# Input and output products of the S5 mixer in other slots, and the last adaLN pieces inside the S5 half of the out-projection

## The chip, the cores and the metric

The kernel runs on 1 core of a Trainium2 chip. The metric is the device time of that core in microseconds (us). The engines are named as in the profile: PE (TensorE matrix products), DVE (VectorE), ACT (ScalarE), POOL (GpSimd) and SP (SyncE, which in this kernel issues nearly all DMAs from one queue, in order).

## The reference

One layer of a diffusion backbone on 640 tokens (128 context, 512 latent) of 2048 columns, all float32. Cut to what matters:

```
mod = silu(c) @ w_ada + b_ada                  # 6 x 2048 columns, for c_ctx and for c
h = rmsnorm(x) * (1 + scale_m) + shift_m
u_a, v_a, u_b = split(h @ w_in)                # 3 x 1024 columns
y_a = u_a * (w_s @ rmsnorm(v_a) + b_s)         # chunk mixer, 8 heads
h_t = lam_bar * h_(t-1) + b_bar @ u_b          # S5: 64 groups of 16 channels, complex
y_b = gelu(Re(c @ h) + d * u_b)                #   states of 64, both directions
y_b = y_b * sigmoid(y_b @ w_glu + b_glu)
mix = [rmsnorm(y_a), rmsnorm(y_b)] @ w_out
x = x + gate_m * rmsnorm(mix)
f = relu(modulate(rmsnorm(x), scale_f, shift_f) @ w_ff1)**2 @ w_ff2
x = x + gate_f * rmsnorm(f)
```

## The kernel before

Most products run as three matrix products of split operands (hi times hi, hi times lo, lo times hi), so each weight chunk is loaded by SP (`wr`), rounded by ACT (`wh`) and subtracted by DVE (`wl`) before PE can take all of it. The modulation (adaLN) is computed in 16 columns (m, c) for gate_m, scale_f, shift_f and gate_f, each of four 1 MB pieces of `w_ada` and a closing step; one call of `ada_step` does one of these (tiles `aw` of 0.5 MB, three buffers, all products of one piece into `adaq`; the closing step makes `adap`).

After a first part (modulation of the input, the S5 quarter `ub` of the in-projection, whose results go to DRAM as `ud`, L322) the program is a hand-written sequence of slots (`slot()`, L488, where every engine keeps the order of the code; the traces give its instructions line 443, since one wrapper issues them). A slot runs its phases in this order: SP loads the chunk after next, `evac`, ACT rounds the next chunk, `act`, `dve`, a first quota of a background flow, DVE subtracts for the next chunk and PE multiplies this one, `pe`, a second quota of the flow, `end`. `at(t, phase, f)` puts a piece of work into slot t. The quotas are in estimated microseconds; the flow is a generator that yields an estimate after each DVE operation.

- Slots 0 to 15: the v columns of the in-projection (48 products of 320 columns a slot, `ws`). The flow is `tables()`: the powers of lam_bar times b, c for 16 units of four groups (`unit(u)`), DVE products on tables St, O and t out of the table tile `big`; small copies ks get two DVE additions a unit, and the results go to DRAM (sd, od, kd).
- Slots 16 to 31: the u columns. `s5_in(u)`, 16 products (`x1p`) a unit, in slots 17 to 21; then the flow is the scan (`scan()`, DVE: scq, sct, X). The chunk mixer follows (vc, z, zt), and its result is stored to DRAM (`yad`) and read back as `ya`.
- Slot 32 has no main chunk. Slots 33 to 48 are the chunk-mixer half of the out-projection (16 chunks of 30 products of 512 columns, `as`).
- Then `s5_out(u)`, 24 products (`yp`) a unit, two units a slot; `y_store` sends y to DRAM (`yd`), `yc_load` reads it back in another layout, `gelu(k)` does GELU (w, yb) and splits the result (yb parts); then 8 chunks of the GLU product.
- `out_b` (L1194): the S5 half of the out-projection (`ob`), for three blocks of tokens (G1) and then two (G2), with the second norm and its transposes (`tp`) between and behind. Here the compiler's scheduler sets the order, no longer the slots. The FFN (L1304) follows and is not touched.

Tiles at the place of the change:

```
w = pa.tile([128, 2, 512], F32, name="aw", tag="aw", bufs=3)      # 0.5 MB each
slot(True, 3.0, 10.0)          # quotas of the flow in slots 0 to 15
```

Of the kernel before, what the change touches and what calls it, by code (L numbers as in the profile page):

```python
# [43 lines left out]
def build(nc, tc, a, out, tap=None):  # L44
# [930 lines left out]
    ya_ = {}  # L975

    def ya_load(k):
        ya_[k] = pbs["pb"].tile([128, L * NJ], F32, name="ya", tag=("ya", "vc")[k % 2], bufs=1)
        SY.dma_start(ya_[k][:, 0:NT], yad[k * 128:(k + 1) * 128])
# [12 lines left out]
    for k, (tl_, pl, ts, ps__) in enumerate(((31, "sp", 31, "end"), (31, "end", 32, "act"), (32, "sp", 33, "act"),  # L992
                                             (33, "sp", 33, "end"), (33, "end", 34, "act"), (34, "sp", 34, "end"))):
        at(tl_, pl, lambda k=k: ya_load(k))
        at(ts, ps__, lambda k=k: split(ya_[k][:, 0:NT], k, g_oa[:, k:k + 1], yah, yal))
# [685 lines left out]
```

## Time and profile before

The three timed runs have a median of 2857.01 us (2856.06 to 2859.68).

| | us |
|---|---|
| profiled execution, its own time | 2859.06 |
| its span, first to last instruction | 2857.2 |
| PE busy | 2661.9 (93%) |
| DVE busy | 1950.0 (68%) |
| ACT busy | 1099.3 (38%) |
| POOL busy | 40.0 (1%) |

The share of the chain that ended last is 77% PE, 9% DVE, 8% DMA. The kernel was read by stages:

| stretch, us | what runs |
|---|---|
| 237.52 to 443.13 | slots 0 to 15, the tables |
| 443.13 to 543.49 | slots 16 to 21 |
| 543.49 to 632.38 | slots 22 to 30 |
| 632.38 to 691.28 | slots 31 to 35 |
| 691.28 to 757.00 | slots 36 to 43 |
| 757.00 to 833.24 | slots 44 to 48, S5 output units 0 to 3 |
| 833.24 to 908.71 | S5 output units 4 to 15 |
| 908.71 to 962.85 | y through DRAM, the last GELU |
| 962.85 to 1021.75 | GLU product |
| 1021.75 to 1222.96 | `out_b`, second norm, transposes |
| 1222.96 to 2857.20 | FFN |

In a row of a stretch stand its bounds, its length, then the busy time with the number of instructions (x) of PE, PEld, DVE, ACT and POOL, the mean granted clock of TensorE (1 is 2.4 GHz, 0.5 is 1.2 GHz), the mean busy share of the 16 DMA engines, and GB/s. In a row of a timeline "[9.77 <-DMA ...]" is the time the engine stood idle ahead of the instruction and what ended it. A row joins xN like instructions, and its length goes from the first start to the last end. A busy matmul row is not a sum to add up: matmuls overlap, so lengths of whole rows or stretches are used.

### The profile page before, as it was taken

Reading aid. Unit: us, or ns where it says so; the run is one execution under the profiler, and the core shown is the slowest. Engines: PE = TensorE matmul, PEld = TensorE weight load, DVE = VectorE, ACT = ScalarE, POOL = GpSimd, SP = SyncE. Lnnn points to the kernel's source line nnn. Section 1 sums busy time; section 2 is a strip of 40 time slices with the busy share of each in tenths; the row PEclk is TensorE's granted clock in tenths of the full one; section 3 lists DMA queues with packets and bytes.
Section 4 is the critical chain, followed back from the end, with each engine's and each line's share of the span. In section 5 each row is a group of like instructions: output and inputs, shape, how many; then the busy total and the mean of one; then the engine's idle time right before and its main releaser. Section 6 shows DMA issues by size and latency. Waiting matters only on the chain.

```text
span 2857.2 us, 42969 instructions
## 1 busy us (share of the span) xinstructions
PE 2661.9 (93%) x17217; PEld 2447.7 (86%) x17217; DVE 1950.0 (68%) x2872; ACT 1099.3 (38%) x1755; POOL 40.0 (1%) x33
## 2 busy tenths in 40 slices
PE   8997888998987898789999999999899999999997
PEld 5687777985665676689999999999899999999996
DVE  5566991478802546677777777777567777777776
ACT  4121321212211334755555555555433222323343
POOL 0000000000000100000000000000000000000000
PEclk9998998999995899899999999999999999999998
DMA  9845779654578565335655555565754455356453
GB/s 304 284 157 203 230 242 222 203 169 171 180 221 174 179 213 206 96 101 176 184 175 178 177 180 178 176 183 177 260 210 147 160 218 200 117 191 219 159 188 114
DMA packets 466567, 537.40 MB, mean 188 GB/s; under 512 B 35216, under 2 KB 378160, under 8 KB 458688
## 3 DMA queue, kind: packets, MB, share of 16 engines
q1 hardware_dynamic: 453264, 528.55, 57.4%
q10 hardware_dynamic: 13104, 6.10, 1.1%
q8 instruction: 136, 2.23, 0.3%
q14 instruction: 63, 0.52, 0.1%
HBM read 417.78 MB, written 116.80 MB: 187 GB/s over the span
## 4 chain that ended last, share of the span: by engine, by line
PE 77%; DVE 9%; DMA 8%; ACT 2%; issue 1%; SPq 1%; ACTq 0%; DVEq 0%
PE X L1304 31%; PE Y L1304 16%; PE Z L1304 8%; PE ws L443 5%; PE ub L186 4%; PE as L443 4%; PE ob L1204 3%; DMA aw<-in_w_ada_dram 2%; PE adaq L443 2%; PE ada L196 2%; DVE t L443 2%; DVE O L443 1%; DVE St L443 1%; PE x1p L443 1%; DMA so<-kd 1%
## 5 line engine op out<-in xcount | busy, mean ns | idle before, releaser
L1291 ACT ACTIVATE wh<-wx 128x1024 fp32r<-128x1024 f32 x223 | 235.8, 1057 | 309.7 <-PE X L1304 141.8
L1296 DVE TENSOR_TENSOR wl<-wx,wh 128x1024 fp32r<-128x1024 f32 x223 | 272.8, 1223 | 73.8 <-ACT wh L1291 71.7
L1304 PE MATMUL X<-B,wh 128*128 128x320 f32 x1376 | 306.5, 310 | 3.3 <-ACT wx L1291 3.3
L1304 PEld LDWEIGHTS X<-B,wh 128*128 128x128 f32 x1376 | 232.3, 190 | 3.5 <-ACT wx L1291 3.5
L1304 PE MATMUL X<-B,wl 128*128 128x320 f32 x688 | 213.2, 310 | 0.0
L1304 PE MATMUL Y<-B,wh 128*128 128x320 f32 x672 | 150.9, 312 | 4.3 <-ACT wh L1291 4.3
L1304 PE MATMUL X<-B,wx 128*128 128x320 f32 x1008 | 154.7, 309 | 0.0
L443 PE MATMUL ws<-hTh,wl 128*128 128x320 f32 x512 | 126.2, 330 | 29.6 <-DVE wl L443 29.6
L443 ACT ACTIVATE wh<-wr 128x1024 fp32r<-128x1024 f32 x56 | 59.3, 1058 | 238.8 <-DMA wr<-in_w_in_dram 138.9
L1304 PEld LDWEIGHTS X<-B,wx 128*128 128x128 f32 x1008 | 149.6, 188 | 0.0
L1379 DVE TENSOR_TENSOR wx<-wx 128x320 fp32r<-128x320 f32 x192 | 93.1, 485 | 78.0 <-ACT wx L1376 78.0
L1502 DVE TENSOR_TENSOR facc<-facc,X 128x640 f32<-128x640 f32 x116 | 95.1, 820 | 73.7 <-PE X L1304 72.8
L443 PE MATMUL adaq<-aw,sc 128*32 128x512 f32 x512 | 95.6, 685 | 52.9 <-DMA aw<-in_w_ada_dram 52.3
L1304 PE MATMUL X<-B2n,wh 128*128 128x320 f32 x608 | 134.7, 309 | 0.0
L443 PE MATMUL ws<-hTh,wh 128*128 128x320 f32 x512 | 128.2, 334 | 7.0 <-ACT wh L443 7.0
L1304 PEld LDWEIGHTS X<-B,wl 128*128 128x128 f32 x688 | 130.2, 189 | 0.0
L443 PE MATMUL ws<-hTl,wh 128*128 128x320 f32 x512 | 124.0, 325 | 0.0
L1291 ACT ACTIVATE wh<-wr 128x1024 fp32r<-128x1024 f32 x76 | 80.4, 1058 | 110.4 <-PE X L1304 51.4
L443 PEld LDWEIGHTS ws<-hTh,wl 128*128 128x128 f32 x512 | 92.4, 203 | 33.2 <-DVE wl L443 33.2
L1291 ACT ACTIVATE wx<-wr 128x1024 fp32r<-128x1024 f32 x75 | 79.3, 1058 | 105.9 <-PE X L1304 54.5
L1291 ACT ACTIVATE wx<-wx 128x1024 fp32r<-128x1024 f32 x74 | 78.3, 1058 | 103.8 <-PE X L1304 45.9
L1304 PEld LDWEIGHTS Y<-B,wh 128*128 128x128 f32 x672 | 114.2, 191 | 4.6 <-ACT wh L1291 4.6
(397 smaller groups left out, 6667.8 us busy)
## 6 DMA issues: line engine op xcount, KB each, us to landing
wx<-in_w_ff_dram SPq DMA_DIRECT2D x169, 512.0 KB
x2d<-wx SPq DMA_DIRECT2D x224, 320.0 KB
aw<-in_w_ada_dram SPq DMA_DIRECT2D x128, 512.0 KB
wr<-in_w_ff_dram SPq DMA_DIRECT2D x87, 512.0 KB
was<-in_w_ada_dram SPq DMA_DIRECT2D x64, 512.0 KB
B2n<-x2d SPq DMA_DIRECT2D x24, 1280.0 KB
wr<-in_w_in_dram SPq DMA_DIRECT2D x48, 512.0 KB
wr<-in_w_out_dram SPq DMA_DIRECT2D x48, 512.0 KB
```

The lines of the kernel that those rows point to most:

```text
L186: T.matmul(p[:, :n], st[:, kk, c:c + 128], mv(k)[:, t0:t0 + n], start=(first and i == 0), stop=(last and i == 2))
L196: T.matmul(p[32 * j:32 * j + 32], sc[:, 2 * (k0 + i):2 * (k0 + i) + 32], w[:, i, :], start=k0 + i < 4, stop=k0 + i >= NK - 4)
L443: return lambda *p, **k: P(f(*p, **k))
L1204: T.matmul(p, st[:, k0 + kk, tsl], mv[:, kk, :], start=(k0 + kk == 0 and i == 0), stop=(k0 + kk == 7 and i == 2))
L1291: P(S.activation(hls[n][0], raw, AF.Copy))
L1296: P(V.tensor_sub(lo, raw, hi.bitcast(F32)))
L1304: P(T.matmul(p, st[:, j, c:c + 128], xv(j, x), start=first and j == 0 and i == 0, stop=j == nj - 1 and i == 2, skip_group_check=not first))
L1379: P(V.tensor_sub(hlt[i][:, 1], raw, hlt[i][:, 0].bitcast(F32)))
L1502: P(V.tensor_add(dst, dst, src))
```

## The change

- The `ud` stores go out from POOL's queue. The loads of the b tables stand right behind the first weight chunk on SP's queue, ahead of the `aw` loads.
- The two sign scalings of b2 and c1 go from DVE to ACT; the two DVE operations a unit on ks become three on POOL (128x16 each), and kd is stored a slot earlier.
- The flow's quotas in slots 0 to 15 go from 13 to 11.3, and `ada_step` is left out in every fourth slot there, and in slots 16 to 20, 33, 34 and every fourth slot from 36 on; slot 32 keeps its three calls; the second calls in slots 42 to 48 go.
- `s5_in` takes four units a slot in slots 17 to 20, and the scan starts in slot 21.
- Of the mixer's results only head 0 goes through DRAM; heads 1 to 5 stay in SBUF (`ykeep`), and their splits move to the ends of slots 32 to 34.
- `s5_rest(e)` starts S5 output in the slot after the scan ends; chunks of the out-projection that are left run beside it.
- The split of yb leaves `gelu` and stands in the first GLU slot.
- The last 6 of the 16 adaLN columns (24 pieces of 1 MB and 6 closing steps) leave the slots; `ada_rest` issues one after each half-block step of `out_b`, from two 1 MB buffers `awr`.

The diff, cut:

```diff
-                nc.sync.dma_start(ud[cb * 128:(cb + 1) * 128], us)
+                nc.gpsimd.dma_start(ud[cb * 128:(cb + 1) * 128], us)
...
+    cols_ = [(m, c) for m in (2, 4, 3, 5) for c in range(4)]
+    steps = [(m, c, q) for m, c in cols_[:10] for q in range(5)]
...
     raw_of(0)
+    for i, nm in enumerate(("b1", "b2")):
+        SY.dma_start(btab[:, i, :], a[nm])
     raw_of(1)
     hi_of(0)
     lo_of(0)
-    ada_load()
     d16 = g_.tile([128, 16], F32, name="d16")
     id16 = g_.tile([128, GH], F32, name="id16")
-    for i, nm in enumerate(("b1", "b2")):
-        SY.dma_start(btab[:, i, :], a[nm])
     SY.dma_start(ctab[:, 0, :], a["c1"])
     SY.dma_start(d16, a["ssm_d"])
     SY.dma_start(id16, a["id16"])
+    ada_load()
...
-        V.tensor_scalar(btab[:, 1, :], btab[:, 1, :], sgn, -1.0, op0=OP.mult, op1=OP.mult)
-        yield 1.3
+        S.activation(btab[:, 1, :], btab[:, 1, :], AF.Copy, scale=nsgn)
...
-        V.tensor_scalar(ctab[:, 0, :], ctab[:, 0, :], sgn, None, op0=OP.mult)
-        yield 1.3
+        S.activation(ctab[:, 0, :], ctab[:, 0, :], AF.Copy, scale=sgn)
...
-            at(now[0] + 1, "dve", lambda: (
-                V.tensor_add(ks[:, 7, :], ks[:, 7, :], ks[:, 15, :]),
-                V.scalar_tensor_tensor(ks[:, 7, :], id16, d16[:, u:u + 1], ks[:, 7, :], op0=OP.mult, op1=OP.add)))
-            at(now[0] + 2, "sp", lambda: SY.dma_start(kd[u], ks[:, 0:15].rearrange("p s c -> p (s c)")))
+            G.tensor_add(ks[:, 7, :], ks[:, 7, :], ks[:, 15, :])
+            G.tensor_tensor(ks[:, 15, :], id16, d16[:, u:u + 1].broadcast_to([128, GH]), op=OP.mult)
+            G.tensor_add(ks[:, 7, :], ks[:, 7, :], ks[:, 15, :])
+            at(now[0] + 1, "sp", lambda: SY.dma_start(kd[u], ks[:, 0:15].rearrange("p s c -> p (s c)")))
...
-        ada_step(t)
-        slot(True, 3.0, 10.0)
+        if t % 4 != 3:
+            ada_step(t)
+        slot(True, 2.0, 9.3)
...
+        if 1 <= h < 6:
+            if h % 2:
+                ykeep.append(pbs["pb"].tile([128, 1536], F32, name="yk", tag="so", bufs=3))
+            y_ = ykeep[-1][:, (h + 1) % 2 * NT:(h + 1) % 2 * NT + NT]
         for n in range(2):
-            V.tensor_mul(zt[:, n * 320:(n + 1) * 320], zt[:, n * 320:(n + 1) * 320], bank["u", h][n][:, :320])
+            V.tensor_mul(y_[:, n * 320:(n + 1) * 320], zt[:, n * 320:(n + 1) * 320], bank["u", h][n][:, :320])
+        if h == 0:
+            at(now[0] + 1, "sp", lambda: SY.dma_start(yad, zt))
+            at(now[0] + 3, "sp", ya_load)
...
-    for t, us in ((17, range(0, 3)), (18, range(3, 6)), (19, range(6, 9)), (20, range(9, 12)), (21, range(12, 16))):
-        for u in us:
-            at(t, "pe", lambda u=u: s5_in(u))
+    for u in range(16):
+        at(17 + u // 4, "pe", lambda u=u: s5_in(u))
...
+    for k in range(6):
+        at((32, 32, 32, 33, 33, 34)[k], "end", lambda k=k: split(ya_[k], k, g_oa[:, k:k + 1], yah, yal))
...
+    def yb_split(k):
+        if k == 0:
+            ybs.extend(a20([128, 8, NT], F32R, f"yb{i}") for i in range(2))
         S.activation(yb_part(k, 0), ybk(k), AF.Copy)
         V.tensor_sub(yb_part(k, 1), ybk(k), yb_part(k, 0).bitcast(F32))
...
+    def s5_rest(e):
+        for u in range(16):
+            at(e + u // 2, "pe", lambda u=u: s5_out(u))
+        for half in range(2):
+            at(e + 4 * half + 4, "sp", lambda half=half: y_store(half))
+            for i in range(4):
+                k = 4 * half + i
+                at(e + 4 * half + 5 + i // 2, "sp", lambda k=k: yc_load(k))
+                at(e + 4 * half + 6 + i // 2, "act", lambda k=k: gelu(k))
...
+    e = None
+    t = 16
+    while t < 49 or e is None or t < e + 11:
+        if t == 21:
+            flow[0] = scan()
+        if 35 <= t < 38:
+            at(t, "end", lambda u=t - 35: so_load(u))
+        if scanned and e is None:
+            e = t
+            s5_rest(e)
         if t == 32:
             for _ in range(3):
                 ada_step(t)
-            slot(False, 0, 3.0)
-            continue
-        if t == 22:
-            flow[0] = scan()
-        ada_step(t)
-        if t >= 41 and t % 2 == 0 or t >= 45:
+            slot(False, 0, 0.0)
+        elif t < 49:
+            if 21 <= t < 32 or t > 34 and t % 4:
+                ada_step(t)
+            slot(True, *((0, 0) if t < 21 else (2.0, 4.6) if t < 32 else (0.0, 2.0) if t == 33 else (2.0, 5.0)))
+        else:
             ada_step(t)
-        if 43 <= t < 46:
-            at(t, "end", lambda u=t - 43: so_load(u))
-        slot(True, *((0, 0) if t < 22 else (1.5, 5.0) if t < 32 else (2.0, 5.0)))
-    while not scanned:
-        ada_step(now[0])
-        slot(False, 0, 7.0)
-    e = now[0]
-    for u in range(16):
-        at(e + u // 2, "pe", lambda u=u: s5_out(u))
-    for half in range(2):
-        at(e + 4 * half + 4, "sp", lambda half=half: y_store(half))
-        for i in range(4):
-            k = 4 * half + i
-            at(e + 4 * half + 5 + i // 2, "sp", lambda k=k: yc_load(k))
-            at(e + 4 * half + 6 + i // 2, "act", lambda k=k: gelu(k))
-    for t in range(e, e + 11):
-        ada_step(t)
-        if t >= e + 8:
-            ada_step(t)
-        slot(False)
-    for t in range(e + 11, e + 19):
-        at(t + 1, "evac", lambda cb=t - e - 11: glu_evac(cb))
+            slot(False, 0, 7.0)
+        t += 1
...
+    for k in range(8):
+        at(t, "act", lambda k=k: yb_split(k))
+    for t in range(t, t + 8):
+        at(t + 1, "evac", lambda cb=cur[0] - 48: glu_evac(cb))
         ada_step(t)
         slot(True)
...
+    awr = fc.tile([128, 5, 1024], F32, name="awr", tag="b6", bufs=1)
+    def ada_rest():
+        pieces = [(m, c, q) for m, c in cols_[10:] for q in range(4)]
+        def ld(i):
+            if i < len(pieces):
+                m, c, q = pieces[i]
+                w = awr[:, 2 * (i % 2):2 * (i % 2) + 2].rearrange("p a (b c) -> p (a b) c", c=512)
+                nc.sync.dma_start(w, wada[:, 4 * q:4 * q + 4, m * D + c * 512:m * D + (c + 1) * 512])
+                return w
+        ws = [ld(0), ld(1)]
+        for i, (m, c, q) in enumerate(pieces):
+            if q == 0:
+                p = pq("adaq")
+            ada_mm(p, ws[i], 4 * q)
+            ws.append(ld(i + 2))
+            yield
+            if q == 3:
+                acc_, cs = awr[:, 4, (c % 2) * 512:(c % 2 + 1) * 512], slice(c * 4, (c + 1) * 4)
+                S.activation(acc_, p, AF.Copy)
+                V.tensor_tensor(modF[:, m - 2, cs, :], ada_cols(pq("adap"), acc_),
+                                bada(m)[:, cs].unsqueeze(2).broadcast_to([128, 4, 2]), op=OP.add)
+                yield
+    rest = ada_rest()
...
+                next(rest, None)
```

The order of instructions shows three places. On SP's queue at the start of the tables stage before (`us` holds the `ub` results, `big` the tables of b and c, `wr` the weight chunks, `aw` adaLN weights):

```order
L322 DMA ud<-us 128x648 x8
L443 DMA wr<-in_w_in_dram 128x8x128 x2
L443 DMA aw<-in_w_ada_dram 128x2x512 x3
L443 DMA big<-in_b_dram 128x2048 x2
L443 DMA big<-in_c_dram 128x2048
L443 DMA d_2092<-in_ssm_d_dram 128x16
L443 DMA id_2093<-in_id_dram 128x16
```

and the same place now:

```order
L445 DMA wr<-in_w_in_dram 128x8x128
L445 DMA big<-in_b_dram 128x2048 x2
L445 DMA wr<-in_w_in_dram 128x8x128
L445 DMA big<-in_c_dram 128x2048
L445 DMA d_2090<-in_ssm_d_dram 128x16
L445 DMA id_2091<-in_id_dram 128x16
L445 DMA aw<-in_w_ada_dram 128x2x512 x3
```

The ud stores are gone from this queue, and the two b loads stand ahead of the second chunk and of three `aw` loads.

On PE at the end of the chunk-mixer half before, the last products of chunk 16, an adaLN piece, and the first S5 output unit:

```order
L443 MATMUL as_6781<-wh_6917,yah_5761 128x512
L443 MATMUL as_6781<-wl_6918,yah_5761 128x512
L443 MATMUL as_6781<-wh_6917,yal_5762 128x512
L443 MATMUL adaq_6900<-aw_6957,sc_85 32x512 x2
L443 MATMUL adaq_6900<-aw_6963,sc_85 32x512 x2
L443 MATMUL yp_7018<-U_4017,so_6668 128x81
L443 MATMUL yp_7018<-X_4016,so_6668 128x81 x2
```

and now, the last products of S5 output unit 1, an adaLN piece, and the first of chunk 16:

```order
L445 MATMUL yp_6829<-U_4002,so_6079 128x81
L445 MATMUL yp_6829<-X_4001,so_6079 128x81 x2
L445 MATMUL adaq_6548<-aw_6693,sc_85 32x512 x2
L445 MATMUL adaq_6548<-aw_6758,sc_85 32x512 x2
L445 MATMUL as_6652<-wh_6775,yah_5724 128x512
L445 MATMUL as_6652<-wl_6776,yah_5724 128x512
L445 MATMUL as_6652<-wh_6775,yal_5725 128x512
```

Units 0 and 1 now stand between chunks 15 and 16; the other 14 still stand behind the last chunk.

On PE in `out_b`, at the same place of G1 (before, one half piece here; ob_8299 to ob_8301 are the three token blocks):

```order
L1204 MATMUL ob_8301<-wh_8304,yg_7615 128x512
L1204 MATMUL ob_8301<-wl_8305,yg_7615 128x512
L1204 MATMUL ob_8301<-wh_8304,yg_7615 128x512
L443 MATMUL adaq_8110<-aw_8147,sc_85 32x512 x2
L1204 MATMUL ob_8299<-wh_8328,yg_7615 128x512
L1204 MATMUL ob_8300<-wh_8328,yg_7615 128x512
```

and now:

```order
L1251 MATMUL ob_8091<-wh_8155,yg_7416 128x512
L1251 MATMUL ob_8091<-wl_8156,yg_7416 128x512
L1251 MATMUL ob_8091<-wh_8155,yg_7416 128x512
L196 MATMUL adaq_7993<-awr_7954,sc_85 32x512 x4
L1251 MATMUL ob_8089<-wh_8184,yg_7416 128x512
L1251 MATMUL ob_8090<-wh_8184,yg_7416 128x512
```

A whole piece of adaLN from an `awr` buffer stands here after each step, 24 pieces in all through G1 and G2.

## Rows read from the trace of the kernel before

**Rows 1.** Work of five stretches (--windows view): columns as in the section on the profile

```profile
237.52:443.13 205.61, 176.02 (x1281) 155.38 (x1281) 178.11 (x271) 52.98 (x123) 10.88 (x6) 0.90 0.76 237
632.38:691.28 58.90, 46.59 (x215) 31.95 (x211) 46.81 (x108) 13.24 (x20) 4.33 (x2) 0.88 0.49 167
833.24:908.71 75.47, 64.36 (x333) 55.93 (x329) 13.40 (x22) 14.32 (x24) 0.00 (x0) 0.61 0.77 213
908.71:962.85 54.14, 27.11 (x105) 11.65 (x104) 19.34 (x30) 11.50 (x17) 0.00 (x0) 0.62 0.79 175
1021.75:1222.96 201.21, 169.91 (x809) 136.68 (x807) 123.64 (x228) 105.66 (x197) 1.57 (x1) 0.90 0.47 164
```

**Rows 2.** Timeline of DVE, 229 to 254 us: start, length, engine, line, operation, [idle before]

```profile
237.49 1.23 DVE L443 TENSOR_TENSOR wl<-wr,wh 128x1024 fp32r<-128x1024 f32 x1 [5.59 <-ACT wh L443]
248.49 1.28 DVE L443 TENSOR_SCALAR big<-big,sgn 128x2048 f32<-128x2048 f32 x1 [9.77 <-DMA big<-in_b_dram]
```

**Rows 3.** Timeline of PE, first and last of 13 waits for DVE

```profile
253.02 0.90 PE L443 MATMUL ws<-hTh,wl 128*128 128x320 f32 x2 [3.95 <-DVE wl L443]
...
417.21 0.56 PE L443 MATMUL ws<-hTh,wl 128*128 128x320 f32 x2 [1.71 <-DVE wl L443]
```

**Rows 4.** Groups of DVE, 262 to 405 us: busy, mean ns, idle before

```profile
L443 DVE TENSOR_TENSOR t<-big 128x576 f32<-128x576 f32 x28 | 23.7, 847 | 0.0
...
L443 DVE SCALAR_TENSOR_TENSOR ks<-id,d,ks 128x16 f32<-128x16 f32 x12 | 2.8, 235 | 0.4
...
L443 DVE TENSOR_TENSOR ks<-ks 128x16 f32<-128x16 f32 x12 | 2.0, 169 | 0.0
```

**Rows 5.** Timeline of all engines, 294 to 298 us

```profile
294.95 1.81 POOL L443 TENSOR_TENSOR diag<-diag,sq 128x640 f32<-128x640 f32 x1 [67.51 <-ACT sq L443]
...
295.27 2.10 DVE L443 TENSOR_TENSOR t<-big 128x576 f32<-128x576 f32 x1
```

**Rows 6.** Timeline of PE in the u half, 443 to 545 us

```profile
465.41 1.92 PE L443 MATMUL adaq<-aw,sc 128*32 128x512 f32 x4 [12.98 <-DMA aw<-in_w_ada_dram]
...
482.62 1.06 PE L443 MATMUL adaq<-aw,sc 128*32 128x512 f32 x8
```

**Rows 7.** Chain of waits, 440 to 560 us: start, length, what

```profile
483.69 7.24 PE ws L443 x48
...
534.53 7.12 PE x1p L443 x64
```

**Rows 8.** Waits of PE, 632.38 to 691.28 us: total, times, longest

```profile
PE as L443 <- DVE yal L443: 3.6, 2, 2.3
PE adaq L443 <- DMA aw<-in_w_ada_dram: 3.5, 3, 2.2
PE as L443 <- DVE zt L443: 3.3, 1, 3.3
```

**Rows 9.** Waits of PE, 691.28 to 833.24 us

```profile
PE adaq L443 <- DMA aw<-in_w_ada_dram: 10.0, 3, 3.9
```

**Rows 10.** Slots 36 to 43, and 44 to the fourth output unit (--windows view)

```profile
691.28:757.00 65.72, 65.72 (x311) 47.96 (x308) 62.56 (x154) 15.47 (x20) 0.00 (x0) 1.00 0.55 186
757.00:833.24 76.24, 65.82 (x333) 44.95 (x332) 22.99 (x54) 14.57 (x20) 0.00 (x0) 0.91 0.61 197
```

**Rows 11.** Chain of waits, 905 to 965 us

```profile
911.93 7.82 DMA yd<-U
919.81 11.38 DMA aw<-in_w_ada_dram
...
960.42 0.75 ACT yb L443
```

**Rows 12.** Groups of PE, 1021.75 to 1222.96 us

```profile
L443 PE MATMUL adaq<-aw,sc 128*32 128x512 f32 x22 | 5.9, 603 | 0.0
```

**Rows 13.** Timelines of SP's queue and of PE, 804 to 812 us

```profile
805.47 1.39 SPq L443 DMA_DIRECT2D aw<-in_w_ada_dram  x3
...
809.31 1.89 PE L443 MATMUL adaq<-aw,sc 128*32 128x512 f32 x4 [3.02 <-DMA aw<-in_w_ada_dram]
```

More of the change, by code (lines that the diff above doesn't have):

```diff
@@ L335, in build @@
     sgn = const("sgn", [128, 1], a["sgn"])
+    nsgn = main.tile([128, 1], F32, name="nsgn")
+    V.tensor_scalar(nsgn, sgn, -1.0, None, op0=OP.mult)
     def gt(name, dt=F32):
@@ L508, in slot @@
         now[0] += 1
-    steps = [(m, c, q) for m in (2, 4, 3, 5) for c in range(4) for q in range(5)]
+    cols_ = [(m, c) for m in (2, 4, 3, 5) for c in range(4)]
+    steps = [(m, c, q) for m, c in cols_[:10] for q in range(5)]
     loads = [(m, c, q, i) for m, c, q in steps if q < 4 for i in range(2)]
@@ L579, in build @@
     vd = dram("vd", [DC, NT])
-    yad = dram("yad", [DC, NT])
+    yad = dram("yad", [128, NT])
     vr = main.tile([128, NTB], F32, name="vr")
@@ L974, in build, with ya_load @@
     at(16, "evac", tables_done)
[L975 to L979, printed above, removed]
+    def ya_load():
+        ya_[0] = pbs["pb"].tile([128, L * NJ], F32, name="ya", tag="ya", bufs=1)[:, 0:NT]
+        SY.dma_start(ya_[0], yad)
     def ya_tiles():
@@ L991, in build @@
     at(32, "pe", acc_tiles)
[L992 to L995, printed above, removed]
+    for k in range(6):
+        at((32, 32, 32, 33, 33, 34)[k], "end", lambda k=k: split(ya_[k], k, g_oa[:, k:k + 1], yah, yal))
     for nb in range(4):
@@ L1045, in gelu @@
         yc = ycs.pop(k)
-        if k == 0:
-            ybs.extend(a20([128, 8, NT], F32R, f"yb{i}") for i in range(2))
         if k % 4 == 0:
@@ L1095, in build @@
                 ada_step(t)
-            slot(False, 0, 3.0)
-            continue
-        if t == 22:
-            flow[0] = scan()
-        ada_step(t)
-        if t >= 41 and t % 2 == 0 or t >= 45:
-            ada_step(t)
-        if 43 <= t < 46:
-            at(t, "end", lambda u=t - 43: so_load(u))
-        slot(True, *((0, 0) if t < 22 else (1.5, 5.0) if t < 32 else (2.0, 5.0)))
-    while not scanned:
-        ada_step(now[0])
-        slot(False, 0, 7.0)
-    e = now[0]
-    for u in range(16):
-        at(e + u // 2, "pe", lambda u=u: s5_out(u))
-    for half in range(2):
-        at(e + 4 * half + 4, "sp", lambda half=half: y_store(half))
-        for i in range(4):
-            k = 4 * half + i
-            at(e + 4 * half + 5 + i // 2, "sp", lambda k=k: yc_load(k))
-            at(e + 4 * half + 6 + i // 2, "act", lambda k=k: gelu(k))
-    for t in range(e, e + 11):
-        ada_step(t)
-        if t >= e + 8:
-            ada_step(t)
-        slot(False)
-    for t in range(e + 11, e + 19):
-        at(t + 1, "evac", lambda cb=t - e - 11: glu_evac(cb))
+            slot(False, 0, 0.0)
[3 more added lines that the diff above has]
+            slot(True, *((0, 0) if t < 21 else (2.0, 4.6) if t < 32 else (0.0, 2.0) if t == 33 else (2.0, 5.0)))
+        else:
+            ada_step(t)
+            slot(False, 0, 7.0)
[4 more added lines that the diff above has]
+        at(t + 1, "evac", lambda cb=cur[0] - 48: glu_evac(cb))
         ada_step(t)
         slot(True)
+    slot(False)
     while steps:
@@ L1137, in build @@
         p_.__exit__(None, None, None)
+    fcc = tc.tile_pool(name="fc", bufs=1, reuse_waits="tile")
+    fc = fcc.__enter__()
+    frr = tc.tile_pool(name="r20", bufs=1, side="right", reuse_waits="tile")
+    r20 = frr.__enter__()
+    awr = fc.tile([128, 5, 1024], F32, name="awr", tag="b6", bufs=1)
[21 more added lines that the diff above has]
+    rest = ada_rest()
     rows = [a20([128, 4, 1024], F32, "rows") for _ in range(2)]
@@ L1222, in build @@
     B1 = [None] * 7
-    fcc = tc.tile_pool(name="fc", bufs=1, reuse_waits="tile")
-    fc = fcc.__enter__()
-    frr = tc.tile_pool(name="r20", bufs=1, side="right", reuse_waits="tile")
-    r20 = frr.__enter__()
     B1[0] = r20.tile([128, 8, 2, NH], F32R, name="B0", tag="r20", bufs=1)
```

10 lines of the change are left out of this document (5 added, 5 removed).

## The prediction

> **What bounds the kernel now.** I read the table of stages first. The FFN (1634 us) is not touched, so what counts are the stages ahead of it, and each has its own limit. I then asked of each stage, in the view of work by stretch, whether PE is busy at full clock; where it is not, the timelines and the waits of PE say what it waits for.
>
> - Tables stage: DVE is busy 178.1 of 205.6 us [rows 1], and PE waits for DVE's `wl` ahead of the chunk of a slot, 13 times, from 253.02 to 417.21 [rows 3]. One slot lasts (417.21 - 253.02) / 12 = 13.68 us. DVE sets this stage. At its start DVE itself stood idle twice, 5.59 us for the first rounded chunk and 9.77 us for the b table [rows 2]; both loads stand on SP's queue behind the ud stores.
> - Slots 16 to 21: PE is the bound except for one wait of 12.98 us for an adaLN load [rows 6].
> - Slots 31 to 35: PE busy 46.6 of 58.9 us at a mean clock of 0.88 [rows 1]; it waits for DVE and for adaLN loads [rows 8].
> - Slots 36 to 43: PE is busy all the time at clock 1.00. From slot 44 on PE is busy 65.8 of 76.2 us at 0.91 [rows 10], and the waits of the whole stretch are 10.0 us for adaLN loads [rows 9], where slots carry two pieces.
> - S5 output, units 4 to 15: PE busy 64.4 of 75.5 us, but at a mean clock of 0.61, with the DMA engines 0.77 busy. y through DRAM: half idle at 0.62 [rows 1]. An adaLN load stands in the chain there with 11.38 us, after a store of 7.82 us [rows 11].
> - `out_b`: PE busy 169.9 of 201.2 us, DMA share 0.47 [rows 1].
>
> **The change part by part**, against the profiled execution (2859.06 us, its span 2857.2 and 1.86 around it). It lies 2.05 us above the median, which is taken off at the end.
>
> 1. Tables stage. The ud stores leave SP's queue, and the b loads no longer stand behind `aw`. So both idle times of DVE at the start can go: 5.59 + 9.77 = 15.4 us. Two sign scalings (1.28 us one [rows 2]) and the two ks operations a unit (0.235 and 0.169 us [rows 4]) leave DVE. By the code a slot holds 16 table operations and one `wl` instead of 17, `wl` and about 1.4 pairs of ks. Of a slot of 13.68 us, 1.23 are wl and 0.6 ks, so an operation is (13.68 - 1.83) / 17 = 0.70 us. The new slot is 16 x 0.70 + 1.23 = 12.4 us: 12 slots x 1.28 = 15.4 us less. The same number of table operations in fewer a slot means that chunk 14 too waits, and the sign scalings cost ACT what they cost DVE; I give back 3 us: -28. Against that stand 48 new operations on POOL, and DVE pays for POOL's company. A product `t<-big` that ran beside an addition of 640 elements on POOL (1.81 us) took 2.10 us [rows 5]; taken over its neighbours' 0.70, that is 1.4 too long. No row shows POOL working on 16 elements. The bounds are 0 and 48 x 1.4 = 67 us. Nearest in size are the 16-element operations on DVE, 0.17 to 0.24 us; if each on POOL holds DVE up for half of that, 48 x 0.1 = 5. I take 5: **-23** (-33 to +34 from these bounds).
>
> The Trainium skill has a rule on this, in SBUF — State Buffer, section "Who interferes with whom": a DVE instruction with two inputs in SBUF contends with a GpSimd instruction that reads SBUF, and the later one stands fully blocked until the first is done. The row agrees: the DVE product begun 0.32 us after POOL's addition outlasted it. By the rule every one of the 48 can cost DVE its whole length, so the term would be -28 + 48 x (length on POOL), at a length like DVE's own -28 + 10 = -18.
>
> 2. Slots 16 to 20. The wait of 12.98 us goes since no adaLN piece is taken there. Five pieces of 1.06 us go, and the one behind the wait ran at half clock (1.92 for half a piece [rows 6]). Four input units a slot instead of three move x1p products and add none: 64 take 7.12 us [rows 7], and ran without a wait in slot 21. What they wait for, the tables from DRAM, comes a slot earlier relative to them; cover is a chunk of 7.24 us [rows 7], and if it fails, one load of some 4 us [rows 13]. **-19** (-12 to -20).
>
> 3. Slots 31 to 35. PE's busy 46.6 us at 0.88 are 41 at full clock. Three pieces less, some 3.2 us, leave 38. Of the 10.4 us of waits [rows 8] the 3.5 for adaLN go, and the other seven shrink, since heads 1 to 5 needn't return from DRAM; I keep 4. 38 + 4 = 42 against 58.9: **-17** (-8 to -22; the low end keeps all DVE waits, since the splits now stand in a row in slot 32).
>
> 4. Slots 36 to 48 and units 0 to 3. Slots 36 to 43 take 65.72 / 8 = 8.2 us each, with PE full; without a piece in every fourth it is 8.0. DVE's 62.56 / 8 = 7.8 in the same slots lies right below, so not less. Behind, 76.24 us before become: slots 44 to 46 at 8.0, two chunks of 7.2 (30 products at the pitch of the 8.2 us slots less a piece of 1.06), four output units of 24 products at the x1p rate (7.12 x 24/64 = 2.67), one piece: 24 + 14.4 + 10.7 + 1.1 = 50. The double pieces with their 10.0 us of waits and the 1.2 GHz behind these are what goes. 1.7 + 26, less 1 for the first table load of the output: **-27** (-15 to -28).
>
> 5. Units 4 to 15. As before two units a slot and one piece a slot; 12 units at 2.67 us would be 32 us, but the stretch takes 75 at clock 0.61. The loads of the output tables go on in the same rate, so I take only **-5** (0 to -25).
>
> 6. y through DRAM. One piece a slot instead of two takes the 11.38 us load out of the chain. But 8 splits of yb, which ran between the GELU steps, now stand in a row ahead of GLU: 8 x 0.75 [rows 11] = 6. **-5.5** (+5 to -10).
>
> 7. `out_b`. 24 pieces of 1.06 us, six closing steps of about the same, minus the 5.9 us that already stood there [rows 12]: 25.4 + 5 - 5.9 = +24.5, PE work that now has no idle PE to hide in. It is the same work that left the stages above, and there it is counted as gone. Their loads, 1 MB each on the queue that also brings w_out, land some 3.8 us after issue for 0.5 MB (issued from 805.47, needed at 809.31 [rows 13]). With two buffers a load has one step of `ob` and the piece behind it to land, about 5 us in G1 and less in G2. Half of them being 1 us late is 12: **+36** (+14 with idle PE used and no wait, +60 at 1.5 us each).
>
> The GLU products and the FFN keep their work: 0. Sum: -23 - 19 - 17 - 27 - 5 - 5.5 + 36 = -60.5, so 2798.6 for the profiled execution, and 2796.5 us against the median.
>
> **The rivals.**
> - (a) PE holds 2.4 GHz in S5 output. There PE does 64.4 us of work at 0.61; with fewer adaLN loads beside, its operands come sooner. For it speaks that the same `yp` stretch is not limited by any engine; against it, that the DMA share of 0.77 is mostly tables, which stay. Term 5 becomes -25: 2776.5, and with `out_b` at its low bound 2755.
> - (b) Pieces in `out_b` late by 2 to 3 us each instead of 0.5: +36 to +60 more, 2833 to 2857. For it: the load row just named. Against: G1's steps have three blocks and the DMA share is only 0.47.
> - (c) POOL's small operations cost DVE 0.6 us each, 24 us more: the tables stage gives its start only, and the time is 2820.
> - (d) Slower. In slots 44 to 48 a piece that came late cost 10.0 / 3 = 3.3 us of waiting [rows 9], and PE then ran at half clock. If each of the 24 pieces costs that and 2.2 us for the slower products behind it, 5.5 x 24 = 132 in place of 12: 2916. The point from which it decides: ahead of `out_b` 96.5 us are saved, less 24.5 of added PE work leaves 72, so 72 / 24 = 3.0 us a piece. Against it: here two loads run ahead, in slots 44 to 48 there was one and a half.
> - The change doesn't do what its words say: by the order 2 of 16 units stand among the out-projection's products, and GELU stands in none. That is already in terms 4 and 5; nothing more is lost by it.
>
> **How the numbers follow.** Forecast 2775 to 2822: 0.52. Rival (a) below 2775: 0.15. (b) 0.13, of it a fifth above 2850. (c) and mishaps of its size, 2815 to 2840: 0.11. (d) 0.06. Something unseen: 0.03, either way. The range from 2757 to 2842 leaves out (d), the tails of (a) and (b). About 0.2% (5.7 us) is what a measurement of this kernel can tell from no change; 2851 to 2863 is met only between (b) and (d): 0.02. Slower 0.07, faster 0.91.
>
> **What would show it.** In the changed profile: DVE's first table operation near 233 instead of 248 (1); the start of slot 16's chunk near 420 and no wait of PE for `aw` until slot 21 (1, 2); no wait for `aw` in slots 36 to 48 and the clock at 1.00 there (4); the `yp` stretch still near 0.6 (5), else (a); in `out_b` waits of `adaq` for `awr`, 24 times some 0.5 us, against 2 to 3 in (b). DVE's table products longer than 0.70 with POOL rows beside them would be (c). The forecast is wrong in its core if the FFN starts later than 1222.96 less 40.

## The result, and the profile after

The changed kernel takes 2789.71 us (2788.33 to 2791.73, four runs) against 2857.7 us of the kernel before in the same four rounds: a ratio of 0.9762, 95% interval 0.9745 to 0.9779. The forecast was 2796.5 us. The span of the profiled execution fell from 2857.2 to 2789.9, by 67.3 us. Single terms were off by up to 14 us and largely cancelled: that the sum came within 7 us of the forecast is luck.

The work by stretch after the change, same columns as [rows 1]; the bounds are the same points of the program as before (start of slots 16, 22, 31, 36, 44, of output unit 4, end of the last output product, start of `out_b`, start of the FFN):

```profile
237.52:425.70 188.18, 165.71 (x1245) 148.28 (x1246) 173.24 (x238) 52.18 (x119) 41.89 (x56) 0.92 0.72 228
425.70:520.37 94.67, 85.52 (x599) 83.61 (x597) 26.30 (x63) 19.20 (x39) 1.99 (x1) 0.87 0.77 179
520.37:607.27 86.90, 81.86 (x580) 74.30 (x576) 74.54 (x175) 19.84 (x41) 9.42 (x5) 1.00 0.53 165
607.27:652.01 44.74, 38.02 (x191) 29.67 (x188) 39.43 (x89) 12.56 (x20) 3.19 (x2) 0.92 0.46 151
652.01:714.64 62.63, 62.63 (x290) 46.48 (x289) 59.63 (x145) 16.14 (x20) 0.00 (x0) 1.00 0.47 157
714.64:763.95 49.31, 49.31 (x275) 39.52 (x272) 26.16 (x61) 12.25 (x18) 0.00 (x0) 1.00 0.56 183
763.95:831.45 67.50, 51.98 (x331) 45.15 (x330) 12.47 (x21) 13.05 (x23) 0.00 (x0) 0.73 0.78 223
831.45:934.17 102.72, 77.51 (x473) 64.25 (x472) 49.05 (x62) 37.75 (x57) 10.66 (x6) 0.80 0.53 139
934.17:1157.71 223.54, 193.55 (x1021) 141.27 (x1019) 125.86 (x233) 110.35 (x205) 1.58 (x1) 0.94 0.71 249
```

Against before: the first ends 17.4 us earlier (425.7 instead of 443.1), and the others are shorter by 5.7 (100.4 before), 2.0 (88.9), 14.2 (58.9), 3.1 (65.7), 26.9 (76.2), 8.0 (75.5) and 10.3 (113.0, the last two rows of the table of stages ahead of `out_b` together); `out_b` is 22.3 longer (201.2), the FFN 2.0 shorter. Together 67.3. PE is busy all the time at clock 1.00 from slot 36 to output unit 3, where it had waited 10.0 us for adaLN loads [rows 9].

DVE at the start of the tables stage (timeline):

```profile
234.12 1.45 DVE L321 TENSOR_TENSOR us<-uacc,ub 128x128 f32<-128x128 f32 x3 [3.59 <-PE ub L186]
237.12 1.42 DVE L321 TENSOR_TENSOR us<-uacc,ub 128x128 f32<-128x128 f32 x3 [1.55 <-DMA ud<-us]
238.46 1.21 DVE L445 TENSOR_TENSOR wl<-wr,wh 128x1024 fp32r<-128x1024 f32 x1
239.59 1.28 DVE L445 TENSOR_TENSOR u<-big 128x512 f32<-128x512 f32 x2
...
265.87 1.23 DVE L445 TENSOR_SCALAR big<-big 128x2048 f32<-128x2048 f32 x1 [4.38 <-DMA big<-in_c_dram]
```

Both waits of [rows 2] are gone, but the last addition of the `ub` stage, which now waits for a ud store, ends at 238.5 (231.9 before), and DVE waits 4.38 us for the c2 table. Behind that a slot takes 12.6 us in the mean from one `wl` to the next, where 13.68 stood before.

PE and SP's queue in slot 17 (timelines; `st` is the table of an input unit, `U` the input u_b read back from `ud`):

```profile
443.01 3.59 PE L445 MATMUL x1p<-U,st__4011 128*128 128x81 f32 x16 [1.91 <-DMA st__4013<-sd]
446.39 3.62 PE L445 MATMUL x1p<-U,st__4013 128*128 128x81 f32 x16
449.81 3.62 PE L445 MATMUL x1p<-U,st__4015 128*128 128x81 f32 x16
460.51 3.67 PE L445 MATMUL x1p<-U,st__4180 128*128 128x81 f32 x16 [7.08 <-DMA st__4180<-sd]
```

```profile
424.10 11.28 SPq L445 DMA_DIRECT2D U<-ud  x8
...
437.61 12.42 SPq L445 DMA_DIRECT2D U<-ud  x8
...
453.87 0.73 SPq L445 DMA_DIRECT2D st__4180<-sd  x1
```

The wait for `aw` [rows 6] went, and the table of the fourth unit is what is late now: its load is issued behind eight U loads. All four units run at half clock (the granted clock is 0.51 from 443.0 to 453.5), 3.6 us instead of 1.8 [rows 7].

### The profile page after: what moved, and what is told of

Its sections match the earlier page's. It is cut to its first block, busy times and chain, and to the rows that moved or that the text cites. A ratio compares the mean times of both kernels' runs of the same rounds, so it can differ in the third digit from the quotient of the medians.

```text
span 2789.9 us, 42919 instructions
## 1 busy us (share of the span) xinstructions
PE 2625.2 (94%) x17217; PEld 2428.4 (87%) x17217; DVE 1942.8 (70%) x2839; ACT 1102.2 (40%) x1757; POOL 73.3 (3%) x89
## 4 chain that ended last, share of the span: by engine, by line
PE 78%; DVE 9%; DMA 7%; ACT 2%; issue 2%; SPq 1%; ACTq 0%; POOL 0%; DVEq 0%; POOLq 0%
PE X L1348 32%; PE Y L1348 16%; PE Z L1348 8%; PE ws L445 5%; PE ub L186 4%; PE as L445 4%; PE ob L1251 3%; PE ada L196 2%; DVE t L445 1%; DVE O L445 1%; DMA wr<-in_w_out_dram 1%; DVE St L445 1%; PE x1p L445 1%; DMA x2d<-wx 1%; PE adaq L445 1%
## 5 line engine op out<-in xcount | busy, mean ns | idle before, releaser
L445 ACT ACTIVATE wh<-wr 128x1024 fp32r<-128x1024 f32 x56 | 59.4, 1060 | 192.5 <-DMA wr<-in_w_in_dram 58.1
L1340 DVE TENSOR_TENSOR wx<-wr,wx 128x1024 fp32r<-128x1024 f32 x75 | 91.8, 1224 | 28.4 <-ACT wx L1335 27.6
```

Of the source, the lines that this page charges most:

```text
L445: return lambda *p, **k: P(f(*p, **k))
L1340: P(V.tensor_sub(lo, raw, hi.bitcast(F32)))
```

## The experiments

Stretches of an experiment are cut at the points named above. The stretch from slot 16 to slot 22 took from 94.2 to 100.8 us in the runs whose edits don't touch it, so differences there of under 7 us say nothing. Each run has one profiled execution.

**1. The ud stores on ACT's hardware queue.**

```
-                nc.gpsimd.dma_start(ud[cb * 128:(cb + 1) * 128], us)
+                nc.scalar.dma_start(ud[cb * 128:(cb + 1) * 128], us)
```

> The changed kernel with the eight ud stores on ACT's hardware queue instead of POOL's software queue. Theory A (the software queue): a store from POOL holds its us buffer longer, and with two buffers the ub stage waits for it; on a hardware queue the last us addition ends at 232 to 234 us instead of 238.5, all behind comes 4 to 6 us earlier, 2784 to 2786 us. Theory B (contention): the b and c loads, which now run at the same time, slow the stores whatever the queue; the last us addition stays at 237 to 239 and the time at 2788 to 2792.

2796.86 us, ratio 0.9778 (0.9761 to 0.9795). The last addition ended at 236.8 us, close to Theory B's 237 to 239 and away from Theory A's 232 to 234: POOL's queue by itself is not it. The time lies above both ranges. ACT's own work came behind its stores here, so that DVE's first table operation began at 241.3, and slots 16 to 21 took 100.8 us, at the long end of what the runs show.

**2. The b and c1 loads behind the `ub` stage**, ud still from POOL.

```
     raw_of(0)
-    for i, nm in enumerate(("b1", "b2")):
-        SY.dma_start(btab[:, i, :], a[nm])
     raw_of(1)
...
     SY.dma_start(id16, a["id16"])
+    for i, nm in enumerate(("b1", "b2")):
+        SY.dma_start(btab[:, i, :], a[nm])
+    SY.dma_start(ctab[:, 0, :], a["c1"])
```

> The changed kernel with the loads of the b tables and c1 behind those of d and id, so that they start behind the ub stage; the ud stores stay on POOL's queue. Theory A (contention: the 3 MB of b and c1 slow the ud stores, for which the us buffers wait): the last us addition ends at 231.5 to 233.5 us, as before, instead of 236.3 to 238.5; DVE's first table operation comes at 244 or later, and slot 16 starts some 3 to 6 us later. Theory B (POOL's software queue is slow by itself): the last us addition stays at 236 or later.

2797.99 us, 0.9789 (0.9774 to 0.9804). DVE (timeline):

```profile
228.14 1.53 DVE L321 TENSOR_TENSOR us<-uacc,ub 128x128 f32<-128x128 f32 x3 [1.97 <-PE ub L186]
231.66 1.48 DVE L321 TENSOR_TENSOR us<-uacc,ub 128x128 f32<-128x128 f32 x3 [1.99 <-PE ub L186]
233.06 1.21 DVE L445 TENSOR_TENSOR wl<-wr,wh 128x1024 fp32r<-128x1024 f32 x1
244.37 1.29 DVE L445 TENSOR_TENSOR u<-big 128x512 f32<-128x512 f32 x2 [10.10 <-ACT big L445]
```

An addition every 3.5 us again (5 in the changed kernel), done at 233.1, also from POOL's queue: it is contention with the early loads, which cost 5.4 us there (238.5 less 233.1). The other 1.2 us to the kernel before already stand ahead of the first addition of the stage, and no run shows why. Slot 16 started at 426.5, where the runs with early loads and ks on POOL started it at 421.3 to 426.2 (experiment 3 aside), so the early loads gain up to 5 us more than they cost, or nothing.

**3. Four us buffers, loads early.**

```
-                us = main.tile([128, L, NJ], F32, name="us", tag="t25", bufs=2)
+                us = p0.tile([128, L, NJ], F32, name="us", tag="us", bufs=4)
```

> The changed kernel with four us buffers instead of two, so that a ud store that lands late holds up no addition; the b and c1 loads stay ahead. Theory A (the two buffers are how the contention reaches PE): the last us addition ends at 231.5 to 233.5 us although the loads run beside it, slot 16 starts 3 to 6 us earlier than in the changed kernel (421.3 to 426.5 in the runs so far), at 417 to 421, and the time is some 4 us below the changed kernel's, a ratio of 0.973 to 0.976 to the kernel before. Theory B (the loads set the start of the tables stage by themselves, by the landing of b2 and c2): the additions end early but DVE's first table operation stays at 236 or later, slot 16 at 421 or later and the ratio at 0.976 or above.

2793.69 us, 0.9778 (0.9765 to 0.9792). The last addition ended at 233.7, DVE's first table operation came at 234.99, and slot 16 started at 419.9, though only 1.4 us below the earliest of the other runs (421.3). That is Theory A up to slot 16; the time isn't, and not for Theory B's reason either. `out_b` took 230.1 us, the others together were 5.9 us shorter. The edit altered the order that the scheduler gives `out_b`:

```profile
927.83:1157.91 230.08, 199.67 (x1021) 146.24 (x1019) 125.81 (x232) 109.63 (x205) 1.58 (x1) 0.90 0.69 242
```

In experiment 1, which has the changed kernel's order of PE, DVE and SP throughout, `out_b` took 223.7. Experiments 2, 3, 4 and 6 got one and the same other order of PE there, and took 228.5, 230.1, 229.8 and 228.1. In their order PE waits up to 1.4 us for a `wh` two or three times, where the longest such wait of the changed kernel is 0.7; in sum that is only 1 to 2 of the 4.5 to 6.5 us, and where the others come from isn't settled. Their total times therefore don't tell what the edit itself is worth; the stretches ahead of `out_b` do.

**4. ks back on DVE.**

```
-            G.tensor_add(ks[:, 7, :], ks[:, 7, :], ks[:, 15, :])
-            G.tensor_tensor(ks[:, 15, :], id16, d16[:, u:u + 1].broadcast_to([128, GH]), op=OP.mult)
-            G.tensor_add(ks[:, 7, :], ks[:, 7, :], ks[:, 15, :])
...
+            at(now[0] + 1, "dve", lambda: (
+                V.tensor_add(ks[:, 7, :], ks[:, 7, :], ks[:, 15, :]),
+                V.scalar_tensor_tensor(ks[:, 7, :], id16, d16[:, u:u + 1], ks[:, 7, :], op0=OP.mult, op1=OP.add)))
...
```

> The changed kernel with the three POOL operations a unit on ks put back as the two on DVE (0.24 and 0.17 us each). Theory A (POOL's operations cost DVE nothing in sum: the six table products have a mean of 0.76 us before and after): DVE gets 32 x 0.2 = 6.4 us more work, slot 16 starts at 430 to 433 us instead of 425.6. Theory B (each POOL operation of 0.6 us holds up a DVE product): the products get shorter and slot 16 starts at 425 or earlier.

2800.72 us, 0.9794 (0.9777 to 0.9812). Slot 16 started at 426.4, inside neither band; in the other runs that have ks on POOL and b early (experiment 3 aside) it started at 421.3 to 426.2. So the part is worth 0 to 5 us. The rest of the difference stands mainly in `out_b` (229.8, in the order of experiments 2, 3 and 6). How POOL and DVE met in the changed kernel, in the tables stage (timeline of both):

```profile
281.75 1.23 DVE L445 TENSOR_TENSOR wl<-wr,wh 128x1024 fp32r<-128x1024 f32 x1
281.98 1.08 POOL L445 TENSOR_TENSOR ks<-ks 128x16 f32<-128x16 f32 x1
...
283.96 1.68 POOL L445 TENSOR_TENSOR diag<-diag,sq 128x640 f32<-128x640 f32 x1 [0.89 <-ACT sq L445]
284.13 2.05 DVE L445 TENSOR_TENSOR t<-big 128x512 f32<-128x512 f32 x1
```

Whoever comes second is held up: POOL's 16 elements lasted until the `wl` begun before them was done (283.0), and DVE's product ended half a microsecond after POOL's 640 were done (285.6). The Trainium skill's rule that the later of the two blocks (SBUF — State Buffer, "Who interferes with whom") agrees with both pairs. A 16-element operation is nearly always the one that waits: the six table products had a mean of 0.76 us before and after (127.6 us in 168, 133.9 in 176, from 262 to 405 us), and 0.76 in this experiment, without these operations on POOL (132.8 in 175). In the second pair it is the long POOL addition that was there before.

**5. Three, four, four, five input units in slots 17 to 20.**

```
-        at(17 + u // 4, "pe", lambda u=u: s5_in(u))
+        at(17 + (u > 2) + (u > 6) + (u > 10), "pe", lambda u=u: s5_in(u))
```

> The changed kernel with three S5 input units in slot 17, then 4, 4, 5 instead of 4, 4, 4, 4. Theory A (three table buffers): the 7.1 us wait of x1p is unit 3, whose table load can only be issued once unit 0 has freed its buffer and stands behind eight U loads; with unit 3 in slot 18 a chunk hides it, the stretch from slot 16 to slot 22 falls from 94.7 to 85 to 88 us and the time to 2780 to 2784. Theory B (the queue): SP's queue with 16 U loads is the bound, the wait only moves to the next unit or to vc, and the time stays at 2787 to 2791.

2789.74 us, 0.9756 (0.9742 to 0.9771): no difference. Waits of PE from slot 16 to slot 22:

```profile
PE vtp L445 <- DMA vc<-vd: 4.9, 1, 4.9
PE x1p L445 <- DMA st__4013<-sd: 3.2, 1, 3.2
PE x1p L445 <- DMA st__4560<-sd: 0.6, 1, 0.6
```

The wait of 7.1 us is gone, and `vc`, which stands behind the same eight loads, is waited for instead.

**6. The second eight U loads at the end of slot 17.**

```
-        u_load(1)
+        at(17, "end", lambda: u_load(1))
```

> The changed kernel with the second half of the U loads (8 of the 16, needed from unit 8 on) issued at the end of slot 17 instead of in front of slot 17's other loads. Theory A (SP's queue is the bound: the loads of unit 3 and of vc stand behind these 8, which take 12.4 us to issue): the waits of 7 to 9 us in slot 17 go, the stretch from slot 16 to slot 22 is 84 to 88 us, the time 2780 to 2784. Theory B (the DMA engines are the bound: the same bytes come later and something else waits): 92 us or more, 2787 to 2791.

2798.04 us, 0.9781 (0.9765 to 0.9797); the stretch took 97.6. In place of the wait of 7.1 us one of 6.6 us came a slot later, behind the same eight loads:

```profile
PE x1p L445 <- DMA st__4305<-sd: 6.6, 1, 6.6
PE x1p L445 <- DMA st__4013<-sd: 3.0, 1, 3.0
```

**7. The second eight U loads in pairs at four places.**

```
+        def ld(tq):
+            SY.dma_start(U[(7 - tq) * GH:(8 - tq) * GH], udv[tq][:, half * HG:(half + 1) * HG, :])
         for tq in range(8):
-            SY.dma_start(U[(7 - tq) * GH:(8 - tq) * GH], udv[tq][:, half * HG:(half + 1) * HG, :])
+            if half == 0:
+                ld(tq)
+            else:
+                at(17 + tq // 4, ("sp", "end")[tq // 2 % 2], lambda tq=tq: ld(tq))
```

> The changed kernel with the second half of the U loads two at a time, at four places from slot 17 to slot 18, with the table loads of the units between them. Theory A (what waits is what stands behind eight U loads in a row, so smaller groups leave no wait over 3 us): the stretch from slot 16 to slot 22 falls from 94.7 to 84 to 89 us. Theory B (the DMA engines carry all of it late, whatever the order): 93 us or more.

2791.05 us, 0.977 (0.9754 to 0.9786). The waits fell to 6.6 us in sum, the longest 3.6, but the stretch took 98.5 us, at a mean granted clock of 0.84. The waits of 2.6 and 3.6 us were each followed by units at 3.6 us instead of 1.8, seven in all; the first:

```profile
441.11 3.67 PE L445 MATMUL x1p<-U,st__4011 128*128 128x81 f32 x16 [2.58 <-DMA st__4013<-sd]
```

Theory A has the waits nearly right and the time wrong. The time is Theory B's; that the DMA engines limit it isn't shown.

**8. One part alone: the tables stage's edits on the kernel before** (ud, b loads, scalings, ks; quotas as before).

```
...
     raw_of(0)
+    for i, nm in enumerate(("b1", "b2")):
+        SY.dma_start(btab[:, i, :], a[nm])
     raw_of(1)
     hi_of(0)
     lo_of(0)
-    ada_load()
...
-            at(now[0] + 1, "dve", lambda: (
-                V.tensor_add(ks[:, 7, :], ks[:, 7, :], ks[:, 15, :]),
...
+            G.tensor_add(ks[:, 7, :], ks[:, 7, :], ks[:, 15, :])
...
         slot(True, 3.0, 10.0)
```

> The kernel before with one part of the change alone: ud stores from POOL, b loads ahead, sign scalings on ACT, ks on POOL; the flow's quotas, adaLN pieces and all later slots as before. Theory A (the tables stage is worth what it gains): slot 16 starts at 428 to 433 us instead of 443.1 and the time is 2843 to 2850. Theory B (what comes behind gives it back: the adaLN load and the U loads of slot 16 come at their own time): the start of slot 22 moves by under 4 us and the time by under 5, 2852 to 2858.

2840.33 us, 0.9932 (0.9917 to 0.9947), 19 us faster; its profiled execution was 14.8 us shorter (2842.4 us). Slot 16 started at 431.0, slot 22 at 535.8 (543.5 before): 12.1 us gained, 4.4 of it given back, to an `aw` wait grown from 12.98 us [rows 6] to

```profile
457.67 1.92 PE L445 MATMUL adaq<-aw,sc 128*32 128x512 f32 x4 [17.36 <-DMA aw<-in_w_ada_dram]
```

Another 8.8 us came between slot 22 and the last output product, where no edit of this run stands; why isn't shown.

**9. No late pieces** (24 pieces and 6 closing steps left out).

```
-    rest = ada_rest()
+    V.memset(modF[:, 1, 8:16], 0.0)
+    V.memset(modF[:, 3], 0.0)
...
-                next(rest, None)
```

> The changed kernel without its 24 late adaLN pieces and 6 closing steps (those columns are zero: this work is left out). Theory A (they are PE work with no cover): 24 x 1.06 + 6 x 0.95 = 31 us and the 3.2 us of waits go, the stretch of out_b and second norm falls from 223.5 to 187 to 192 us, the time to about 2756. Theory B (they partly fill time in which PE waited anyway, for DVE's wl and in the transposes): the stretch stays at 198 to 206, the time at 2765 to 2773.

2761.83 us, 0.9653 (0.9638 to 0.9669). `out_b` took 195.6 us, 27.9 less than with the pieces: between the two theories. PE's waits there, of 0.8 us or more:

```profile
PE tp L1283 <- ACT hf L1285: 20.4, 9, 14.6
PE ob L1252 <- DVE wl L176: 5.6, 6, 3.3
PE tp L1283 <- DVE diag L1240: 4.9, 2, 4.3
PE tp L1283 <- ACT hg L1285: 1.3, 1, 1.3
PE ob L1252 <- ACT wh L175: 0.9, 1, 0.9
```

**10. All late products, two loads** (22 loads of 1 MB left out).

```
-            ws.append(ld(i + 2))
+            ws.append(ws[i])
```

> The changed kernel with all products of the late pieces, but loads of the first two alone (the others multiply the same two tiles: 22 loads of 1 MB are left out). Theory A (the price of a late piece is its PE time): only the 3.2 us of waits for awr go, 2785 to 2789 us. Theory B (the loads hold up those of w_out on the same queue): 10 us or more go, 2780 us or less.

2781.92 us, 0.9729 (0.9713 to 0.9745), between the two theories; `out_b` 215.8 us:

```profile
PE tp L1283 <- ACT hf L1285: 19.7, 11, 13.0
PE tp L1283 <- ACT hg L1285: 1.3, 1, 1.3
PE ob L1251 <- DVE wl L176: 0.9, 2, 0.6
PE tp L1283 <- DVE diag L1239: 0.6, 1, 0.6
```

By these two runs the 27.9 us are 20.2 for the products and 7.7 for the loads. That split is rough: the scheduler gave this run another order too, and another order went with up to 6.5 us in `out_b` (experiment 3). For the late loads themselves PE waited 3.2 us in the changed kernel:

```profile
PE adaq L196 <- DMA awr<-in_w_ada_dram: 3.2, 4, 1.5
```

The products add 30 us of busy PE (192.5 against 162.5), and 9 of the 10.5 us for which PE waited for `wl` and `diag` without them are gone: about a third of the added work filled waits that were there.

**11. No adaLN pieces in the slots of S5 output** (behind GLU instead).

```
         else:
-            ada_step(t)
             slot(False, 0, 7.0)
```

> The changed kernel without adaLN pieces in the slots of S5 output from the second on (slots 49 to 57; they come behind the GLU product, which costs time there, so only the stretch of units 4 to 15 is read: 67.6 us at a clock of 0.73 in the changed kernel). Theory A (rival (a) of the prediction: fewer adaLN loads beside the table loads let PE run faster): the stretch falls to 50 to 56 us and the clock rises above 0.9. Theory B (the tables of the output units come one at a time and set the pace by themselves): 63 to 68 us, clock below 0.8.

2792.38 us (two runs), 0.9763 (0.9742 to 0.9784). Units 4 to 15 took 58.8 us (67.5 in the changed kernel); the row of the stretch, and the waits of PE there:

```profile
759.83:818.61 58.78, 49.19 (x290) 47.48 (x288) 12.29 (x20) 11.96 (x21) 0.00 (x0) 0.68 0.65 185
```

```profile
PE yp L445 <- ACT U L445: 8.0, 1, 8.0
PE yp L445 <- DMA so<-kd: 1.1, 3, 0.6
PE yp L445 <- DMA so<-od: 0.2, 1, 0.2
```

The tables of the output units (`so`) were waited for 7.7 us in the changed kernel and 1.3 here; the clock, 0.68, did not rise from 0.73. The runs whose edits don't touch the stretch took 63.1 to 67.5 us in it, so 4 to 9 us were adaLN loads beside table loads, less than rival (a) had, and not by the clock. `out_b`, which carries part of these pieces here, took 232.8 us.

**12. The split of yb back in each GELU step.**

```
-    for k in range(8):
-        at(t, "act", lambda k=k: yb_split(k))
...
+        yb_split(k)
```

> The changed kernel with the split of yb back in each GELU step instead of in a row in the first GLU slot. Theory A (the last four GELU steps are a chain of ACT and DVE that ends last, and each split lengthens it by some 1.4 us): the stretch from the last output product to the out-projection goes from 102.7 to 105 to 108 us, the time up by 3 to 6. Theory B (the eight splits in a row are what PE waits for: the first GLU chunk took 11.2 us instead of 7.3): the stretch falls to 97 to 100 us, the time by 3 to 5.

2800.41 us, 0.9801 (0.9779 to 0.9823); the stretch took 106.1 us instead of 102.7 (100.8 to 102.8 in the runs whose edits don't touch it). Theory A: the split is better behind the GELU steps. Behind the last adaLN load these steps took 19.8 us instead of 13.6, but GLU's products then took 60.9 instead of 66.3; most of the 3.4 us lies ahead of that load.

## Why the prediction was right, step by step

| step | forecast, us | measured, us |
|---|---|---|
| 1 tables stage | -23 | -17.4 |
| 2 slots 16 to 21 | -19 | -5.7 |
| slots 22 to 30 | 0 | -2.0 |
| 3 slots 31 to 35 | -17 | -14.2 |
| 4 slots 36 to 48, units 0 to 3 | -27 | -30.0 |
| 5 units 4 to 15 | -5 | -8.0 |
| 6 y through DRAM, with GLU | -5.5 | -10.3 |
| 7 `out_b` | +36 | +22.3 |
| FFN | 0 | -2.0 |
| sum | -60.5 | -67.3 |

- Step 1: the mechanism held, with sizes off both ways. A slot took 12.6 us where 12.4 was forecast. DVE's first table operation came at 239.6 instead of 233: the last addition of the `ub` stage ended 6.6 us later, 5.4 of them because the early b loads slowed the ud stores and with them the two `us` buffers (experiments 2 and 3). The working gave the earlier loads no cost. The wait for c2 (4.4) was not seen either. The 5 us for POOL did not come (experiment 4). -23 + 6.5 + 4.4 - 5 = -17; that it closes so well is luck, since slot 16 started up to 4.3 us sooner in other runs of the same stage. Two numbers of the working don't follow from it: with POOL's bounds of 0 and 67 us the range around -28 is -28 to +39, and rival (c) would leave nothing of the stage's gain, not its start.
- Step 2 is where the working failed: "if it fails, one load of some 4 us". The wait for `aw`, to 465.4, had covered 16 U loads, as SP's queue before shows:

```profile
436.27 7.28 SPq L443 DMA_DIRECT2D U<-ud  x8
...
446.00 10.93 SPq L443 DMA_DIRECT2D U<-ud  x6
...
460.38 5.00 SPq L443 DMA_DIRECT2D U<-ud  x2
```

  Now 9.0 us of waits stand there, and PE's products behind them run at half clock. The gain of 5.7 us is near the best case: the other runs that leave the stretch alone gained from 0 to 6. Experiments 5 to 7 show that the order of these loads moves the wait to another tile or into the clock. Experiment 8, which keeps the adaLN pieces, shows the same place taking time back.
- Step 3: PE's busy time came as forecast (38.0 us). The waits fell to 6.7 us and not to 4, and 2.6 of them are for an `aw` load that was counted as gone.
- Step 4 held, by the trace: no wait, clock 1.00. The size lies 2 us beyond the range given for it. No run made this part, the largest gain, or step 3 by itself.
- Step 5: a part of rival (a). The clock rose from 0.61 to 0.73 and PE's busy time fell from 64.4 to 52.0 us, while its waits grew by 4.4; which part of the change did it no run shows. Fewer adaLN loads shorten the stretch, but not by the clock (experiment 11).
- Step 6 came near by two misses, which is luck. The load of 11.38 us, which was to leave the chain, is still in it (chain of waits):

```profile
831.95 5.25 DMA yd<-U
837.26 11.36 DMA aw<-in_w_ada_dram
```

  Taking it out gives little by itself. In experiment 11, without adaLN loads there, the store of y stands in its place, and GLU's products run on from 34.8 us behind the last output product instead of 36.4:

```profile
821.96 11.21 DMA yd<-U
```

  The splits of yb, counted as 6 us of cost, were a gain of some 3 us (experiment 12). Against before, the chain reaches the load 5.3 us sooner, has 4.8 us less adaLN work on PE behind it, and its last GELU steps take 13.6 us instead of 20.6; GLU, forecast at 0, takes 6.6 us longer, since some of its products had run between those steps.
- Step 7: some 7.7 us for loads where 12 were taken (experiment 10, roughly), and of the 31 us of products, a third in PE's old waits; "no idle PE to hide in" was wrong. From 27.9 the half pieces that stood in `out_b` before come off: 27.9 - 5.6 = 22.3. Rivals (b) and (d) had priced the loads at 2 to 5.5 us a piece; by experiment 10 they cost 0.35 (7.7 / 22).

The gain ahead of the FFN is thus mainly slots 31 to 48, S5 output and the tables stage; it was paid for with 22 us in `out_b`.

## What to carry to other kernels

When a wait is to go, look up what else was being loaded behind it: a wait of 13 us for one tile had covered other loads that took 23 us to issue, and at most 6 us came back. Work added to a stage costs less than its busy time where PE waits there for other engines, so count those waits before adding it up. When a load is to leave a chain, look up what stands right behind it: here a store took its place. When small edits are compared in a program whose scheduler orders a later part, compare stage by stage, and first see how far a stage moves in runs that leave it alone: in experiment 3 a lead of 6 us was lost in another order of `out_b`, 500 us later.

## What the runs showed of the hardware

- A DVE operation with two operands in SBUF and an operation on POOL held each other up in both directions: a 16-element POOL addition took 1.08 us behind a `wl`, where 0.22 us was the shortest of its kind, and a DVE product took 2.05 us beside POOL's 1.68.
- Short waits can cost more in clock than in waiting. In experiment 7 the waits were 6.6 us in 98.5, but seven units behind them ran 16 products in 3.6 us instead of 1.8, and the mean granted clock was 0.84, below the 0.91 of the kernel before, which had waited 13 us once. It doesn't always come so: in experiment 12 the first three units ran at full clock behind a wait of 2.5 us:

```profile
439.13 1.98 PE L445 MATMUL x1p<-U,st__4011 128*128 128x81 f32 x16 [2.46 <-DMA st__4013<-sd]
```

- Loads beside the ud stores held these up from POOL's queue and from ACT's (experiment 1). With 3 MB of b and c1 loads the additions that wait for the ud stores came every 5 us, and without these loads every 3.5, from the same queue (experiment 2).
